# Values of the dilated attention: 512 weight columns per matmul, four PSUM banks held over K pairs

## The chip, the cores and the metric

The kernel runs on one core of a Trainium2 chip. The metric is the device time in microseconds (us). Before the change three runs gave 2682.06, 2686.4 and 2687.64 us; the median is 2686.4 us.

A core has TensorE (PE; its loads of stationary weights are a second row, PEld), VectorE (DVE), ScalarE (ACT), GpSimd (POOL) and SyncE (SP), which issues all DMAs of this kernel in one queue.

## The reference

Two networks of two layers each, one after the other, on a sequence of 512 with 1024 features. The change is in both layers of the first one. There a layer normalizes x to h, multiplies h by `w_in`, and feeds two attentions; cut to what matters here:

```python
p = h @ w_in[layer]                       # h is 512 x 1024
c_q, c_kv, k_r, gate_a, dil_qkv, gate_b = jnp.split(p, split_points, axis=-1)
...
qkv = dil_qkv.reshape(B, S, 3, 3, 8, 64)  # 3 groups, q/k/v, 8 heads of 64
for g, (window, dil) in enumerate(((128, 1), (512, 4), (2048, 16))):
    v = qkv[:, :, g, 2]                   # 512 x 512: the values of group g
    o, lse = banded_attention(to_strided(q, dil), to_strided(k, dil), to_strided(v, dil), ...)
```

So a layer needs three products of 512 x 1024 by 1024 x 512, the values of the three groups. Group 0 uses the rows of v in order; groups 1 and 2 use them with every fourth row together (`to_strided`).

## The kernel before

Everything is kept with features on the 128 partitions: `hh` and `hl` are the high and the low part of h, each [128, 8, 512], where the middle index k counts the eight blocks of 128 features and the last one the tokens. A weight block is loaded as `wraw`, split by ACT into a high part (`whi`, line 75) and by DVE into the rest (`wlo`, line 76), and a product is three matmuls (`mm3`, lines 128 to 132): high by high (L130), high by low (L131), low by high (L132). In the trace's names `out<-a,b` the first name is the operand that streams and the second the stationary one.

For the values the stationary operand is h itself (128 tokens of one feature block), and the weights stream, so that tokens come out on the partitions. Four such sets of 128 tokens, i in the order 1, 2, 3, 0, make up the 512. In group 0 a set is a run of 128 neighbouring tokens (for i = 0 the two ends, copied by POOL into `endq` and `endk`). In groups 1 and 2 set i is `slice(i, 512, 4)`: every fourth token, so the stationary operand is read from `hh` and `hl` with a step of four 4-byte elements.

The loop (lines 564 to 584) runs over six half groups z of 256 weight columns; for each it prefetches the next one's weights (`slabs`, two transfers of 512 KB, alternately in the `whi`/`wlo` buffers and in two buffers `wv`), calls `c.side(VS[z])`, and for each i runs 8 x 3 matmuls into one PSUM bank (`pgv`, pool `pg` of two banks). ACT then scales the result into `v0` or `v12` (line 584).

`c.side(n)` takes n steps of a filler: a step loads 512 KB of another network's modulation weights (`adaw`, line 727) and DVE reduces them (line 728). There are 24 such steps in a layer, and `VS` says how many are placed at which z. The tiles `adaw` use the buffers of `q0` and `k0`, of which `endq` and `endk` hold one each until group 0 is done.

A scheduler puts the instructions of each engine in order when the kernel is built; semaphores then keep the dependences, and each engine runs its own list in order. The matmuls before this stage belong to the other attention (its last product is `po`, line 532), and the scheduler puts some `pgv` matmuls between those. After the stage come the products of q and k (`pg`, weights `in_w_dqk_dram`).

Of the kernel before, what the change touches and what calls it, by code (L numbers as in the profile page):

```python
# [10 lines left out]
F32, F32R, BF16, I32 = dt.float32, dt.float32r, dt.bfloat16, dt.int32  # L11
AF = mybir.ActivationFunctionType
# [5 lines left out]
S = 512  # L18
D = 1024
KD = 8  # L20
# [395 lines left out]
def block1_mixers(c, l, nm, mixf, side, w0, fill):  # L416
    nc, tc = c.nc, c.tc
    hh, hl, rb, rc = nm.hh, nm.hl, nm.rb, nm.rc
    I = c.ins
    W = I["w_in"][l]  # L420
    if True:
# [23 lines left out]
        with ExitStack() as e2:  # L445
# [11 lines left out]
            for ct in range(6):  # L457
                ps = c.gemm(W[:, ct], hh, hl, w=w0.pop(0) if w0 else None, pool=(c.px, "px") if ct in PX else None)
# [15 lines left out]
            for k in (3, 4, 0, 1, 2):  # L474
                t = cf[:, k, :]
# [4 lines left out]
            scale = float(96.0 ** -0.5)  # L480
            khl = [[mp.tile([128, 2, S], F32R, name=f"k{z}{i}") for z in "hl"] for i in range(2)]
            for p in range(4):

                kh, kl = khl[p % 2]
                ps = c.gemm(I["w_uk"][l][:, p], ch[:, 3:5], cl[:, 3:5], 2)
# [9 lines left out]
                for e in range(2):  # L495
                    ps = c.gemm(I["w_uq"][l][:, 2 * p + e], ch, cl, 3)
# [5 lines left out]
                    if (p, e) == (0, 0):  # L502
                        uvh, uvl = c.wslab(I["w_uv"][l], [128, 2, 512])
                        vm = mp.tile([128, 4, 512], F32, name="vm")
                        for i in range(4):
                            ps = (c.px if i in UV else c.pg).tile([128, S], F32, name="pv", tag="px" if i in UV else "pg")
# [29 lines left out]
        with ExitStack() as e2:  # L536
            dp = c.pool(e2, "dil", side)
# [8 lines left out]
            v0 = dp.tile([128, 4, 512], F32, name="v0")  # L546
            v12 = dp.tile([128, 2, 4, 512], F32, name="v12")
            V = I["w_dv"][l]
            ends = [dp.tile([128, KD, 128], F32R, name=f"end{t}", tag=t, bufs=2) for t in ("q0", "k0")]
# [3 lines left out]
            tags = cycle(("q0", "k0"))  # L553
            c.fill.append(fill(lambda: dp.tile([128, 1024], F32, name="adaw", tag=next(tags), bufs=2)))

            def slabs(z):
                ws = []
                for hf in range(2):
                    t = dp.tile([128, 2, 4, 256], F32R, name="wv", tag="qk12", bufs=2) if z % 2 else None
                    ws.append(c.wslab(V[:, z, 4 * hf:4 * hf + 4], [128, 4, 256], out=t and (t[:, 0], t[:, 1])))  # L560
                return ws

            wn = slabs(0)
            for gi in range(3):
                for s in range(2):
                    z = 2 * gi + s
                    wv = wn
                    if z < 5:
                        wn = slabs(z + 1)
                    c.side(VS[z])  # L570
                    cs = slice(256 * s, 256 * s + 256)
                    for i in (1, 2, 3, 0):
                        if gi:
                            h, t, j = (hh, hl), slice(i, 512, 4), 8 + i
                        elif i:
                            h, t, j = (hh, hl), slice(128 * i - 64, 128 * i + 64), 3 + i
                        else:
                            h, t, j = ends, slice(0, 128), 7
                        ps = c.pg.tile([128, 256], F32, name="pgv", tag="pg")
                        for k in range(KD):  # L580
                            wh, wl = wv[k // 4]
                            c.mm3(ps, h[0][:, k, t], h[1][:, k, t], wh[:, k % 4, :], wl[:, k % 4, :], k == 0, k == KD - 1)
                        dst = v0[:, i, cs] if gi == 0 else v12[:, gi - 1, i, cs]
                        nc.scalar.activation(dst, ps, AF.Copy, scale=rc[:, j:j + 1])  # L584
            qk = {}
            top, low = slice(0, 64), slice(64, 128)

# [1012 lines left out]
def build(tc, I, out):  # L1600
    nc = tc.nc
    with ExitStack() as es:
# [62 lines left out]
        for l in range(2):  # L1665
            ex.close()
            prev = nm
            with ExitStack() as em:
                xp = c.pool(em, "mixf", B)
                mixf = xp.tile([128, KD, S], F32, name="mixf")  # L1670
                prev.factors(xp)

                def fill(place):
                    nonlocal sc
                    sc = sc or silu_c(ap)
                    return adaln(c, sc, 0, l, place)

                block1_mixers(c, l, prev, mixf, B, w0 if l == 0 else None, fill)
                mp = c.pool(em, "mp", B)
                if l == 0:  # L1680
                    x = load_x(Scaled, gvec(I["norm_g"][1]))
                else:
                    x = load_x(Norm, *modulation(c, 0, 0, final_g), [I["w_rw"][:, k] for k in range(3)], final_g)
                c.out_proj(mp, I["w_out"][l], 0, [mixf[:, k] for k in range(KD)], x, norm=nm)
            xd = to_dram(xT)
# [195 lines left out]
HB = {0: (0,), 3: (1, 2, 3)}  # L1881
XE = lambda nc: nc.vector
CT = 8
VS = (0, 4, 4, 5, 4, 6)
GT = ((0, 1, 2, 3), (), ())
PX = (2, 3)
UV = (0, 1)
# [60 lines left out]
def slab(w, n=128):  # L1948

    K, N = w.shape  # L1950
    return np.ascontiguousarray(w.reshape(K // 128, 128, N // n, n).transpose(1, 2, 0, 3))


def feat(v):

    v = np.asarray(v)
    return np.ascontiguousarray(np.swapaxes(v.reshape(v.shape[:-1] + (v.shape[-1] // 128, 128)), -1, -2))


def layout_block1(inp):  # L1960
    o = {}
    o["x"] = np.ascontiguousarray(np.asarray(inp["x"])[0].T.reshape(KD, 128, S).transpose(1, 0, 2))
    o["norm_g"] = feat(inp["norm_g"])
    o["final_g"] = feat(inp["final_g"])
    o["qkv_g"] = np.ascontiguousarray(np.concatenate([feat(inp["q_norm_g"]), feat(inp["kv_norm_g"])], -1))
    swp = np.concatenate([np.arange(16, 32), np.arange(0, 16)])
    w_in, w_uk, w_uv, w_uq, w_dv, w_gate, w_dqk, w_out = ([] for _ in range(8))
    for l in range(2):
        w = np.asarray(inp["w_in"][l])
        kr = w[:, 640:672]  # L1970
        w_in.append(slab(np.concatenate([w[:, 0:640], kr, kr, kr[:, swp], kr[:, swp]], 1)))
        w_gate.append(slab(np.concatenate([w[:, 672:1184], w[:, 5792:6304]], 1)))
        dil = w[:, 1184:5792].reshape(1024, 3, 3, 8, 64)
        w_dv.append(slab(np.concatenate([dil[:, g, 2].reshape(1024, 512) for g in range(3)], 1), 256))
        w_dqk.append(slab(np.concatenate([dil[:, g, j, 2 * p:2 * p + 2].reshape(1024, 128)
                                          for p in range(4) for g in range(3) for j in range(2)], 1)))
        ukv = np.asarray(inp["w_ukv"][l]).reshape(256, 8, 128)
        w_uk.append(slab(ukv[:, :, 0:64].reshape(256, 512), 128))
        w_uv.append(slab(ukv[:, :, 64:].reshape(256, 512), 512)[:, 0])
        uq = np.asarray(inp["w_uq"][l]).reshape(384, 8, 96)  # L1980
        cols = []
        for h in range(8):
            n, r = uq[:, h, :64], uq[:, h, 64:]
            cols += [n, r, r[:, swp]] if h % 2 == 0 else [r, r[:, swp], n]
        w_uq.append(slab(np.concatenate(cols, 1)))
        w_out.append(slab(np.asarray(inp["w_out"][l])))
    for k, v in (("w_in", w_in), ("w_uk", w_uk), ("w_uv", w_uv), ("w_uq", w_uq), ("w_dv", w_dv), ("w_gate", w_gate),
                 ("w_dqk", w_dqk), ("w_out", w_out)):
        o[k] = np.stack(v)
    return o  # L1990
# [60 lines left out]
```

## Time and profile before

| | |
|---|---|
| median of three runs | 2686.4 us |
| profiled execution, its own time | 2683.97 us |
| its span | 2682.2 us |
| PE busy | 2589.2 us (97%) |
| DVE, ACT, POOL busy | 63%, 40%, 8% |
| from the last `po` to the first product of q and k, layer 1 | 172.59 to 281.28 us |
| the same, layer 2 | 743.56 to 852.25 us |

A matmul's record has a start that is measured and an end that is modelled, so that records overlap. How fast PE goes is therefore read from the distance between starts.

### The profile page before, as it was taken

How to read it: one execution, taken by the hardware profiler on the slowest of the kernel's cores; microseconds unless marked ns; L12 is line 12 of the kernel's file. 1: busy time of each engine (PE TensorE's matmuls, PEld its weight loads, DVE VectorE, ACT ScalarE, POOL GpSimd, SP SyncE). 2: the span in 40 equal slices, each digit the busy share in tenths (PEclk: the TensorE clock that was granted, in tenths of full speed). 3: DMA queues.
4: the chain of work that ended last, by engine and by line, in shares of the span. 5: the costliest groups of instructions: out<-in, count | busy, mean ns of one | idle time of the engine just before them, and what ended most of it. 6: DMA issues, size and time to landing. Idle time of an engine off the chain costs nothing.

```text
span 2682.2 us, 40139 instructions
## 1 busy us (share of the span) xinstructions
PE 2589.2 (97%) x15813; PEld 2101.0 (78%) x15813; DVE 1685.4 (63%) x3362; ACT 1068.4 (40%) x1923; POOL 220.0 (8%) x311
## 2 busy tenths in 40 slices
PE   8999999999999999999999989899999989999998
PEld 6779877787699777786777777777888867888887
DVE  5773567555844766558668678688454697553544
ACT  5651344434622334554344373532232423432331
POOL 0000111000000111021101123200000210200000
PEclk9999999999999999999998988899999999999999
DMA  4144111241252221331221233388333402233322
GB/s 145 43 166 159 55 56 56 65 144 53 92 189 94 58 61 56 115 99 52 61 72 49 78 111 107 102 260 259 117 95 106 151 26 75 81 89 99 95 82 83
DMA packets 91880, 265.18 MB, mean 99 GB/s; under 512 B 14372, under 2 KB 26924, under 8 KB 90796
## 3 DMA queue, kind: packets, MB, share of 16 engines
q1 hardware_dynamic: 91692, 262.61, 31.3%
q8 instruction: 125, 2.05, 0.3%
q14 instruction: 63, 0.52, 0.1%
HBM read 246.06 MB, written 16.52 MB: 98 GB/s over the span
## 4 chain that ended last, share of the span: by engine, by line
PE 80%; DVE 10%; issue 3%; DMA 3%; ACT 2%; POOL 2%; SPq 0%; ACTq 0%; DVEq 0%; POOLq 0%
PE pg L130 16%; PE pg L131 16%; PE pg L132 16%; PE pgv L132 3%; PE pgv L130 3%; PE pgv L131 3%; DMA adaw<-in_ada_w_dram 2%; DVE wlo L76 2%; PE po L692 1%; PE po L532 1%; PE tp L527 1%; PE sc L632 1%; PE po L697 1%; PE phs L1371 1%; POOL hl L344 1%
## 5 line engine op out<-in xcount | busy, mean ns | idle before, releaser
L130 PE MATMUL pg<-hh,whi 128*128 128x512 f32 x1560 | 632.2, 405 | 9.2 <-ACT whi L124 6.5
L131 PE MATMUL pg<-hl,whi 128*128 128x512 f32 x1560 | 630.5, 404 | 0.0
L132 PE MATMUL pg<-hh,wlo 128*128 128x512 f32 x1560 | 628.4, 403 | 0.3 <-DVE wlo L76 0.3
L75 ACT ACTIVATE whi<-wraw 128x1024 fp32r<-128x1024 f32 (+3 forms) x358 | 335.6, 938 | 695.9 <-PE pg L131 561.1
L76 DVE TENSOR_TENSOR wlo<-wraw,whi 128x1024 fp32r<-128x1024 f32 (+4 forms) x354 | 406.7, 1150 | 295.0 <-ACT whi L75 289.4
L130 PEld LDWEIGHTS pg<-hh,whi 128*128 128x128 f32 x1560 | 295.9, 190 | 86.1 <-ACT whi L124 6.5
L131 PEld LDWEIGHTS pg<-hl,whi 128*128 128x128 f32 x1560 | 296.6, 190 | 76.5 <-issue 7.5
L132 PEld LDWEIGHTS pg<-hh,wlo 128*128 128x128 f32 x1560 | 296.4, 190 | 76.4 <-issue 6.1
L130 PE MATMUL pg<-hidh,whi 128*128 128x512 f32 (+1 forms) x396 | 147.3, 372 | 0.0
L131 PE MATMUL pg<-hidl,whi 128*128 128x512 f32 (+1 forms) x396 | 146.7, 370 | 0.0
L132 PE MATMUL pg<-hidh,wlo 128*128 128x512 f32 (+1 forms) x396 | 146.1, 369 | 0.0
L728 DVE CUSTOM_DVE_ANT_0 adaw<-adaw,sc 128x1024 f32<-128x1024 f32 x96 | 116.6, 1225 | 44.4 <-DMA adaw<-in_ada_w_dram 37.3
L600 POOL TENSOR_TENSOR shf<-shf,roped 128x512 f32<-128x512 f32 x48 | 61.9, 1289 | 622.0 <-ACT whi L75 339.1
L584 ACT ACTIVATE v<-pgv,rsy 128x256 f32<-128x256 f32 x48 | 22.8, 474 | 166.7 <-PE pgv L132 162.8
L132 PEld LDWEIGHTS pg<-hidh,wlo 128*128 128x128 f32 x396 | 74.4, 188 | 14.5
L130 PEld LDWEIGHTS pg<-hidh,whi 128*128 128x128 f32 x396 | 74.4, 188 | 14.2
L641 ACT ACTIVATE pp<-pp,nm 128x256 f32<-128x256 f32 x128 | 63.5, 497 | 54.6 <-DVE nm L638 54.6
L131 PEld LDWEIGHTS pg<-hidl,whi 128*128 128x128 f32 x396 | 74.4, 188 | 13.7
L131 PE MATMUL pgv<-wlo,hh 128*128 128x256 f32 x240 | 83.9, 350 | 0.0
L130 PE MATMUL pgv<-whi,hh 128*128 128x256 f32 x240 | 83.9, 350 | 0.0
L132 PE MATMUL pgv<-whi,hl 128*128 128x256 f32 x240 | 83.6, 348 | 0.0
L1541 ACT ACTIVATE fu<-fu 128x512 f32<-128x512 f32 x44 | 27.8, 632 | 112.6 <-DVE fu L754 112.6
(540 smaller groups left out, 4947.9 us busy)
## 6 DMA issues: line engine op xcount, KB each, us to landing
adaw<-in_ada_w_dram SPq DMA_DIRECT2D x96, 512.0 KB, 4.6
wraw<-in_ffn_up_dram SPq DMA_DIRECT2D x88, 512.0 KB, 3.6
wraw<-in_w_dqk_dram SPq DMA_DIRECT2D x48, 512.0 KB, 3.5
wraw<-in_ffn_down_dram SPq DMA_DIRECT2D x32, 512.0 KB, 3.6
wraw<-in_w_dv_dram SPq DMA_DIRECT2D x24, 512.0 KB, 3.8
wraw<-in_w_gate_dram SPq DMA_DIRECT2D x16, 512.0 KB, 3.7
wraw<-in_w_out_dram SPq DMA_DIRECT2D x16, 512.0 KB, 3.8
wraw<-in_w_hg_dram SPq DMA_DIRECT2D x16, 512.0 KB, 3.7
```

Of the source, the lines that this page charges most:

```text
L75: nc.scalar.activation(hi, raw, AF.Copy)
L76: (eng or nc.vector).tensor_tensor(lo, raw, hi.bitcast(F32), op=ALU.subtract)
L130: mm(out, lhsT=ah, rhs=bh, start=first, stop=False)
L131: mm(out, lhsT=ah, rhs=bl, start=False, stop=False)
L132: mm(out, lhsT=al, rhs=bh, start=False, stop=last)
L344: nc.gpsimd.tensor_tensor(self.hl[:, k, t], u, h, op=ALU.subtract)
L527: nc.tensor.transpose(tp[:, kt, :], pe[:, kt * 128:(kt + 1) * 128], c.ident)
L532: nc.tensor.matmul(po[64 * e:64 * e + 64], lhsT=vm[:, kt, p * 128 + 64 * e:p * 128 + 64 * e + 64], rhs=pts[e][:, kt, :], start=kt == 0, st ...
L600: nc.gpsimd.tensor_tensor(sh, sh, roped[:, 1, :], op=ALU.mult)
L641: nc.scalar.activation(pz, pz, AF.Exp, bias=nm[:, z, i:i + 1], scale=0.125, accum_out=st[:, 1, z, i:i + 1])
L728: nc.vector.tensor_tensor_reduce(w, in0=w, in1=sc, scale=1.0, scalar=0.0, op0=ALU.mult, op1=ALU.add, accum_out=mod[:, j:j + 1])
L1541: nc.scalar.activation(u, u, AF.Silu)
```

## The change

The values of a group are now made in one go: each matmul streams 512 weight columns instead of 256. The loop runs over the three groups and, inside, over four K pairs (`kp`, two feature blocks each); the weights of a pair are one transfer of 512 KB in the ordinary `whi`/`wlo` buffers. Since all four sets i are still open when the next pair comes, four PSUM banks are held over the group: those of `pg` and `px` for groups 0 and 2, those of `py` and `pz` for group 1. ACT evicts the four banks at the end of a group. The weights are laid out in blocks of 512 columns, and `VS` now has twelve entries.

```diff
-            def slabs(z):
-                ws = []
-                for hf in range(2):
-                    t = dp.tile([128, 2, 4, 256], F32R, name="wv", tag="qk12", bufs=2) if z % 2 else None
-                    ws.append(c.wslab(V[:, z, 4 * hf:4 * hf + 4], [128, 4, 256], out=t and (t[:, 0], t[:, 1])))
-                return ws
-
-            wn = slabs(0)
             for gi in range(3):
-                for s in range(2):
-                    z = 2 * gi + s
-                    wv = wn
-                    if z < 5:
-                        wn = slabs(z + 1)
-                    c.side(VS[z])
-                    cs = slice(256 * s, 256 * s + 256)
+                pools = ((c.pg, "pg"), (c.px, "px")) if gi % 2 == 0 else ((c.py, "py"), (c.pz, "pz"))
+                ps = [pools[i // 2][0].tile([128, S], F32, name="pgv", tag=pools[i // 2][1]) for i in range(4)]
+                for kp in range(4):
+                    wh, wl = c.wslab(V[:, gi, 2 * kp:2 * kp + 2], [128, 2, S])
+                    c.side(VS[4 * gi + kp])
                     for i in (1, 2, 3, 0):
                         if gi:
-                            h, t, j = (hh, hl), slice(i, 512, 4), 8 + i
+                            h, t = (hh, hl), slice(i, 512, 4)
...
-                        ps = c.pg.tile([128, 256], F32, name="pgv", tag="pg")
-                        for k in range(KD):
-                            wh, wl = wv[k // 4]
-                            c.mm3(ps, h[0][:, k, t], h[1][:, k, t], wh[:, k % 4, :], wl[:, k % 4, :], k == 0, k == KD - 1)
-                        dst = v0[:, i, cs] if gi == 0 else v12[:, gi - 1, i, cs]
-                        nc.scalar.activation(dst, ps, AF.Copy, scale=rc[:, j:j + 1])
+                        for j in range(2):
+                            k = 2 * kp + j
+                            c.mm3(ps[i], h[0][:, k, t], h[1][:, k, t], wh[:, j, :], wl[:, j, :], k == 0, k == KD - 1)
+                for i in (1, 2, 3, 0):
+                    j = 8 + i if gi else 3 + i if i else 7
+                    nc.scalar.activation(v12[:, gi - 1, i] if gi else v0[:, i], ps[i], AF.Copy, scale=rc[:, j:j + 1])
...
-VS = (0, 4, 4, 5, 4, 6)
+VS = (0, 2, 2, 2, 2, 2, 2, 2, 2, 3, 2, 2)
```

The built order changes in this stage of the two layers and in the end of the attention before it; elsewhere all engines' lists are the same. Three places follow, each from the first layer.

SP's queue from the first `adaw` transfer to the second transfer for q and k, before:

```order
L727 DMA adaw<-in_ada_w_dram 128x1024 x2
L67 DMA wraw<-in_w_dv_dram 128x1024
L727 DMA adaw<-in_ada_w_dram 128x1024
L67 DMA wraw<-in_w_dv_dram 128x1024
L727 DMA adaw<-in_ada_w_dram 128x1024 x2
L67 DMA wraw<-in_w_dv_dram 128x1024
L727 DMA adaw<-in_ada_w_dram 128x1024 x3
L67 DMA wraw<-in_w_dv_dram 128x1024
L727 DMA adaw<-in_ada_w_dram 128x1024 x5
L67 DMA wraw<-in_w_dv_dram 128x1024 x2
L727 DMA adaw<-in_ada_w_dram 128x1024 x10
L67 DMA wraw<-in_w_dqk_dram 128x1024
```

and now:

```order
L718 DMA adaw<-in_ada_w_dram 128x1024 x2
L67 DMA wraw<-in_w_dv_dram 128x1024 x2
L718 DMA adaw<-in_ada_w_dram 128x1024 x2
L67 DMA wraw<-in_w_dv_dram 128x1024
L718 DMA adaw<-in_ada_w_dram 128x1024 x12
L67 DMA wraw<-in_w_dv_dram 128x1024
L718 DMA adaw<-in_ada_w_dram 128x1024 x3
L67 DMA wraw<-in_w_dv_dram 128x1024
L718 DMA adaw<-in_ada_w_dram 128x1024 x2
L67 DMA wraw<-in_w_dv_dram 128x1024
L718 DMA adaw<-in_ada_w_dram 128x1024 x2
L67 DMA wraw<-in_w_dqk_dram 128x1024
```

Six of the twelve `w_dv` transfers of the layer stand ahead of these rows in both. Of the other six, three (the last three K pairs of group 2) now come behind a run of twelve `adaw` transfers.

ACT's list from the first split after the attention (`whi` and `wv` are splits of weights, `v` are evictions), before:

```order
L75 ACTIVATE wv<-wraw 128x1024 x2
L584 ACTIVATE v_1512<-pgv,rsy 128x256 x3
L75 ACTIVATE whi<-wraw 128x1024
L584 ACTIVATE v_1512<-pgv,rsy 128x256 x4
L75 ACTIVATE wv<-wraw 128x1024
L75 ACTIVATE whi<-wraw 128x1024
L584 ACTIVATE v_1512<-pgv,rsy 128x256
L75 ACTIVATE wv<-wraw 128x1024
L584 ACTIVATE v_1513<-pgv,rsy 128x256 x3
```

and now:

```order
L75 ACTIVATE whi<-wraw 128x1024 x3
L575 ACTIVATE v_1512<-pgv,rsy 128x512 x4
L75 ACTIVATE whi<-wraw 128x1024 x3
L575 ACTIVATE v_1513<-pgv,rsy 128x512 x4
L75 ACTIVATE whi<-wraw 128x1024 x4
L575 ACTIVATE v_1513<-pgv,rsy 128x512 x2
L75 ACTIVATE whi<-wraw 128x1024
L575 ACTIVATE v_1513<-pgv,rsy 128x512 x2
```

The evictions of a group now stand in one run (the last one in two). The splits for the next group's first two pairs stand ahead of group 0's run, the split for group 2's first pair ahead of group 1's run.

PE at the end of group 2 and the first product of q and k (numbers are tiles: `pgv_1824` is set i = 0), before:

```order
L130 MATMUL pgv_2259<-wv_2042,hh_103 128x256
L131 MATMUL pgv_2259<-wv_2042,hh_103 128x256
L132 MATMUL pgv_2259<-wv_2042,hl_104 128x256
L130 MATMUL pg_2299<-hh_103,whi_2291 128x512
L131 MATMUL pg_2299<-hl_104,whi_2291 128x512
```

and now:

```order
L130 MATMUL pgv_1824<-whi_1941,hh_103 128x512
L131 MATMUL pgv_1824<-wlo_1942,hh_103 128x512
L132 MATMUL pgv_1824<-whi_1941,hl_104 128x512
L130 MATMUL pg_1993<-hh_103,whi_1985 128x512
L131 MATMUL pg_1993<-hl_104,whi_1985 128x512
```

Width and buffers have changed; the order of the two stages has not. The bank given to `pg_1993` is that of set i = 1 (`pgv_1825`), the first of the four to be finished and evicted.

## Rows read from the trace of the kernel before

**Rows 1.** The page: busy time of PE, and the chain by engine and line.
```profile
PE 2589.2 (97%) x15813; PEld 2101.0 (78%) x15813; DVE 1685.4 (63%) x3362; ACT 1068.4 (40%) x1923; POOL 220.0 (8%) x311
...
PE 80%; DVE 10%; issue 3%; DMA 3%; ACT 2%; POOL 2%; SPq 0%; ACTq 0%; DVEq 0%; POOLq 0%
PE pg L130 16%; PE pg L131 16%; PE pg L132 16%; PE pgv L132 3%; PE pgv L130 3%; PE pgv L131 3%; DMA adaw<-in_ada_w_dram 2%; DVE wlo L76 2%; PE po L692 1%; PE po L532 1%; PE tp L527 1%; PE sc L632 1%; PE po L697 1%; PE phs L1371 1%; POOL hl L344 1%
```
**Rows 2.** Windows: attention's end, then the stage in both layers (columns named in the header).
```profile
core 0: us, PE busy (x) PEld busy (x) DVE busy (x) ACT busy (x) POOL busy (x), PEclk, DMA share, GB/s
151.40:172.59 21.19, 21.10 (x116) 12.67 (x114) 12.77 (x34) 13.87 (x29) 1.05 (x2) 1.00 0.40 150
172.59:281.28 108.69, 108.69 (x545) 108.69 (x545) 44.95 (x65) 20.73 (x33) 0.00 (x0) 1.00 0.48 165
743.56:852.25 108.69, 108.69 (x545) 108.69 (x545) 44.80 (x64) 20.74 (x33) 0.00 (x0) 1.00 0.49 165
```
**Rows 3.** Timeline of PE, group 0, 256 columns (start us, length us).
```profile
182.06 0.28 PE L130 MATMUL pgv<-wv,hh 128*128 128x256 f32 x1
...
182.77 0.28 PE L130 MATMUL pgv<-wv,hh 128*128 128x256 f32 x1
```
**Rows 4.** The same, group 1: 256 columns, stationary operand with step four.
```profile
211.97 0.40 PE L130 MATMUL pgv<-whi,hh 128*128 128x256 f32 x1
...
212.67 0.40 PE L130 MATMUL pgv<-whi,hh 128*128 128x256 f32 x1
```
**Rows 5.** The same, first product of q and k: 512 columns, no step.
```profile
281.28 0.39 PE L130 MATMUL pg<-hh,whi 128*128 128x512 f32 x1
...
281.98 0.39 PE L130 MATMUL pg<-hh,whi 128*128 128x512 f32 x1
```
**Rows 6.** Windows of the `pgv` instructions alone: groups 1 and 2 of layer 1.
```profile
191.67:281.28 89.61, 89.61 (x386) 89.57 (x384) 7.58 (x16) 1.00 0.46 158
```
**Rows 7.** Timeline of PEld: line 378, one streamed column; without step, then step four.
```profile
21.75 1.53 PEld L378 LDWEIGHTS pst<-ones,sqa 128*128 128x128 f32 x13
...
23.51 1.94 PEld L378 LDWEIGHTS pst<-ones,sqa 128*128 128x128 f32 x8
```
**Rows 8.** The instructions of the tile `pst` of line 378: shortest/median/longest in ns.
```profile
L378 PEld LDWEIGHTS pst<-ones,sqa x52: 133/192/330, 21.5 to 591.6; 128*128 128x128 f32 x44, 128*64 128x64 f32 x8
```
**Rows 9.** Groups by line, 172.6 to 281.3 us: busy us, mean ns, idle before.
```profile
L728 DVE CUSTOM_DVE_ANT_0 adaw<-adaw,sc 128x1024 f32<-128x1024 f32 x24 | 28.8, 1221 | 8.2 <-DMA adaw<-in_ada_w_dram 8.1
L584 ACT ACTIVATE v<-pgv,rsy 128x256 f32<-128x256 f32 x23 | 10.9, 475 | 78.2 <-PE pgv L132 76.3 <-PE po L532 1.9
L76 DVE TENSOR_TENSOR wlo<-wraw,whi 128x1024 fp32r<-128x1024 f32 x6 | 7.3, 1225 | 24.7 <-ACT whi L75 24.7
L75 ACT ACTIVATE whi<-wraw 128x1024 fp32r<-128x1024 f32 x6 | 6.3, 1051 | 3.3 <-PE pgv L132 3.3
```
**Rows 10.** Groups of ACT, 140 to 172 us: a copy of 512 columns out of PSUM.
```profile
L528 ACT ACTIVATE ptm<-tp 128x512 f32<-128x512 f32 x14 | 8.3, 598 | 8.2 <-PE tp L527 8.2
```
**Rows 11.** DMA view, 172.6 to 281.3 us: GB/s in 40 slices, total, issue to landing (us).
```profile
GB/s 0 193 176 216 274 270 238 240 342 338 381 366 369 274 3 14 304 345 302 0 0 6 0 0 193 176 309 317 341 15 0 193 6 188 5 193 0 0 0 0
DMA packets 4901, 17.90 MB, mean 165 GB/s; under 512 B 544, under 2 KB 544, under 8 KB 4896
...
adaw<-in_ada_w_dram SPq DMA_DIRECT2D x22, 512.0 KB, 5.0
```
**Rows 12.** Windows, layer 1: GB/s is the last column.
```profile
200.00:220.00 20.00, 20.00 (x87) 20.00 (x87) 10.52 (x17) 2.61 (x5) 0.00 (x0) 1.00 0.67 249
```
**Rows 13.** SP's queue: timeline, and waits of 172.6 to 281.3 (us, times, longest).
```profile
202.59 39.41 SPq L727 DMA_DIRECT2D adaw<-in_ada_w_dram  x10
...
SPq L727 <- DVE mod L728: 55.1, 20, 17.0
```

More of the change, by code (lines that the diff above doesn't have):

```diff
@@ L572, in block1_mixers @@
                     for i in (1, 2, 3, 0):
                         if gi:
-                            h, t, j = (hh, hl), slice(i, 512, 4), 8 + i
+                            h, t = (hh, hl), slice(i, 512, 4)
                         elif i:
-                            h, t, j = (hh, hl), slice(128 * i - 64, 128 * i + 64), 3 + i
+                            h, t = (hh, hl), slice(128 * i - 64, 128 * i + 64)
                         else:
-                            h, t, j = ends, slice(0, 128), 7
@@ L579, in block1_mixers @@
-                        ps = c.pg.tile([128, 256], F32, name="pgv", tag="pg")
-                        for k in range(KD):
-                            wh, wl = wv[k // 4]
-                            c.mm3(ps, h[0][:, k, t], h[1][:, k, t], wh[:, k % 4, :], wl[:, k % 4, :], k == 0, k == KD - 1)
-                        dst = v0[:, i, cs] if gi == 0 else v12[:, gi - 1, i, cs]
-                        nc.scalar.activation(dst, ps, AF.Copy, scale=rc[:, j:j + 1])
+                            h, t = ends, slice(0, 128)
@@ L1973, in layout_block1 @@
         dil = w[:, 1184:5792].reshape(1024, 3, 3, 8, 64)
-        w_dv.append(slab(np.concatenate([dil[:, g, 2].reshape(1024, 512) for g in range(3)], 1), 256))
+        w_dv.append(slab(np.concatenate([dil[:, g, 2].reshape(1024, 512) for g in range(3)], 1), 512))
         w_dqk.append(slab(np.concatenate([dil[:, g, j, 2 * p:2 * p + 2].reshape(1024, 128)
```

## The prediction

> **What bounds the kernel now.** I read the page first: PE is busy for 97% of the span and holds 80% of the chain that ended last; in its list by line the products of the values (`pgv`) stand behind those of the shared product helper (`pg`), with 3% for each of their three lines [rows 1]. So PE's own time is what a change must cut. Then the windows of the two stages that the change touches: 108.69 us in each layer, PE and PEld busy throughout, granted clock 1.00 (the 2.4 GHz level), DMA at half its share, DVE 45 us and ACT 21 us busy [rows 2]. Nobody makes PE wait there.
>
> What PE does in that time is read from starts. In group 0, where the stationary operand is contiguous, six matmuls of 256 columns take 0.71 us: 118 ns each [rows 3]. In groups 1 and 2, where it is read with a step of four elements, three take 0.70 us: 233 ns each, for the same 256 columns [rows 4]. A matmul of 512 columns with a contiguous stationary operand also takes 233 ns [rows 5]. So in groups 1 and 2 something other than the columns sets the pace. Line 378 says what: it streams a single column per matmul, and its loads follow each other by (1.53 - 0.19) / 12 = 112 ns when contiguous and by (1.94 - 0.33) / 7 = 230 ns with a step of four [rows 7]; the lengths of one load, 192 and 330 ns, are those of its own group [rows 8]. A strided load takes about 233 ns whether one column or 256 stream beside it. PE in groups 1 and 2 is bound by loads, and half of its streaming time is empty: 384 loads in 89.61 us [rows 6].
>
> **The change part by part**, for one layer; both layers have the same counts and the same 108.69 us.
>
> *Groups 1 and 2.* Before: 2 groups x 2 halves x 4 sets x 8 blocks x 3 = 384 matmuls, each with its load, 89.6 us [rows 6]. After: 2 x 4 sets x 8 blocks x 3 = 192, with 512 columns. No row shows a strided load beside 512 columns. Lower bound: the longer of load and stream, 233 ns [rows 4, 5], 44.8 us. Upper bound: none of the second 256 columns is hidden, 233 + 117 = 350 ns, 67.2 us. I take 234.5 ns, near the lower end: the nearest row is the contiguous case, where a load of 112 ns beside a stream of about 117 gives 118 [rows 3, 7], so two nearly equal lengths cost a nanosecond over the longer one. 192 x 234.5 = 45.0 us; the term is -44.6 us (bounds -44.8 and -22.4).
>
> The Trainium skill ("TensorE: Matmul & The Clock Gate", LDWEIGHTS) gives a load as columns / 1.2, an estimate of 107 ns for these 128, with no word of a step. By it loads would be hidden in 118 ns already, halving their number would gain nothing, and the sum would be about 0. The rows say otherwise, 230 ns [rows 7], and decide.
>
> *Group 0.* 192 x 118 ns = 22.6 us become 96 x 233 ns = 22.4 us: -0.2 us [rows 3, 5].
>
> *Evictions.* 24 of 475 ns [rows 9] become 12 of 512 columns, each like ACT's 598 ns copy [rows 10]. ACT is busy for 20.73 of 108.69 us, and in a group the bank of i = 1 is finished three sets (18 matmuls, 4.2 us) before the last. Group 1 has banks of its own, so PE does not stop between groups. Group 2 needs group 0's banks back, a whole group (22 us) later. The first product of q and k takes the bank of i = 1, free by then: 0. Had it been the last bank, it would be 0.6 us and a semaphore.
>
> *Weights.* The same 12 transfers and splits. A transfer now feeds 24 matmuls of 0.2345 us, 5.6 us of PE; before it fed 48, 5.7 us in group 0 and 11.2 in groups 1 and 2. The list of SP now has twelve `adaw` transfers ahead of the second pair of group 2. Worked by hand, from the end of group 0 as zero: ACT evicts until 0.8, splits group 1's third pair until 1.9, DVE follows until 3.1 and can only then reduce again. DVE's reductions (1.2 us each [rows 9]) and the splits, which wait for a weight buffer that PE frees every 5.6 us, then stand in turn: split at 6.8 to 8.0, three reductions to 11.8, split to 13.6, six reductions to 21. SP issues the twelfth `adaw` at 16.1, when the one four back is reduced, and the weights right behind it; with about 4 to 5 us to land [rows 11] they are there at 21. ACT is then busy with group 1's evictions until 23.2, splits until 24.3, DVE until 25.5. PE needs them at 22.5 + 5.6 = 28. The margin is 2.5 us; the pairs behind have 3 to 5. So 0, with up to 5 us if supply is thin: 17.90 MB [rows 11] in 61 us are 294 GB/s; slices of the stage reach 338 to 381 [rows 11].
>
> *The end of the attention before.* There 32 matmuls of 256 columns (3.8 us) filled PE's gaps; now 28 of 512 (6.5 us) do, and DVE and ACT do the same three splits in another place. All of this is counted in the terms above if the gaps have no room; PE is busy for 21.10 of 21.19 us there [rows 2], modelled ends included, so little room. If the 2.7 us all fitted, that would be -2.7. If the splits, now earlier, push the softmax chain, at most one more of each is in its way (1.05 + 1.22 us [rows 9]): +2.3. I take +0.5.
>
> *Sum.* -44.6 - 0.2 + 0.5 = -44.3 us a layer, -88.6 us for two. Against the profiled execution's own 2683.97 us (span 2682.2 and 1.8 around it) that is 2595.4; the median of the runs is 2.4 above that execution, so 2597.8 us.
>
> **The rivals.**
>
> 1. *Load and stream hide each other only in part.* 233 ns for 256 columns is also 2 x 117. If a strided load of 117 ns ran ahead of its stream instead of beside it, 512 columns would take 350 ns, and the layer would gain 22.4 + 0.2 - 0.5 = 22.1 us: 2642 us. Against it: with one column the distance is 230 ns too [rows 7], where the sum would be about 117. The Trainium skill ("TensorE: Matmul & The Clock Gate", The mechanism) says that a load overlaps a running matmul only when they use different row groups, which would put every load here in series. By that rule, the trace disagrees: contiguous loads of 112 ns and streams of 117 make 118 together [rows 3, 7].
>
> 2. *Supply becomes the bound.* All of the stage's 17.90 MB now have to come in 61 us. At the 249 GB/s of one stretch of the stage before [rows 12] they take 71.9, which is 11.0 more a layer: 2 x 33.3 = 66.6 us gained, 2620 us. For it: DVE already waits 8.1 us for `adaw` [rows 9], and only four buffers hold them, two until group 0 is done. Against it: 249 is a stretch in which SP waited for DVE, not for the engines.
>
> 3. *Slower: the twelve `adaw` issues in a row.* PE's second pair of group 2 stands behind them in SP's queue. The row of ten before took 39.4 us, 3.9 per issue, and SP waited 55.1 us for DVE's reductions in 20 waits, 17.0 at longest [rows 13]. At 3.9 the weights would be issued 44 us after group 0 and ready at 51, 23 us late, which eats half of the gain. The run begins 3.3 us before the end of group 0, and landing and splits take 5.0 + 1.05 + 1.14, so from (28 + 44.3 - 7.2 + 3.3) / 12 = 5.7 us per issue the kernel is slower than before. If every second issue waited as long as the longest, 8.5 each, PE would stand still for 78 us, 34 more than the gain: 2684 + 67 + 2 = 2753 us. Against it: these waits were paced by weight buffers, of which PE freed one per 11.2 us; it now frees one per 5.6.
>
> 4. *No change*, 2686 us: loads are not what sets the pace in groups 1 and 2 (233 ns would then belong to the columns read there, and 512 of them would take 467), against the 230 ns beside one column [rows 7]. The rule on a load's length in the Trainium skill, above, would come out here too.
>
> **How the numbers follow.** Forecast 0.82, rival 1 0.05, rival 2 (any part of it) 0.09, rival 3 0.02, rival 4 0.02. The forecast's own range: at best 44.8 + 0.2 + 2.7 = 47.7 a layer, 2591 us, at worst 44.6 + 0.2 - 2.3 - 3 = 39.5, 2607; the runs shown spread by 4 us below their median, so it begins at 2588. To leave no more than 2 in 10 outside, the range takes in rival 2 and ends at 2622. About 0.2% (5 us) is what a measurement of this kernel tells from no change. Faster by more: all but rivals 3 and 4, 0.96; within it: rival 4, 0.02; slower: rival 3, 0.02.
>
> **What would show it.** Right: the distance between `pgv` starts in groups 1 and 2 stays at 233 to 236 ns with 512 columns; from the last `po` to the first product of q and k there are about 61 us instead of 108.69, granted clock 1.00; PE is nowhere idle in it; the rest of the program has its old lengths. Wrong: starts 300 ns or more apart (rival 1); idle PE ahead of the second to fourth K pair of group 2, released by `wlo` or `whi`, with SP waiting for DVE (rivals 2 and 3); the attention's end, 21.19 us before, longer by more than 5 us; or a granted clock below 1.00 in a stage where it was not.

## The result, and the profile after

The changed kernel takes 2590.61 us (median of four runs, 2589.3 to 2591.42), the kernel before 2685.08 us: a ratio of 0.9648, 95% interval 0.9631 to 0.9665. The forecast was 2597.8 us. The profiled execution took 2591.42 us, with a span of 2589.6.

The page of the profile after, PE's busy time and the chain by engine and line, which answer to [rows 1]:

```profile
PE 2495.2 (96%) x15237; PEld 1999.1 (77%) x15237; DVE 1685.8 (65%) x3362; ACT 1063.7 (41%) x1899; POOL 219.6 (8%) x311
...
PE 82%; DVE 9%; ACT 2%; issue 2%; DMA 2%; POOL 2%; SPq 0%; ACTq 0%; DVEq 0%; POOLq 0%
PE pg L130 18%; PE pg L131 18%; PE pg L132 18%; DMA adaw<-in_ada_w_dram 2%; PE pgv L130 2%; PE pgv L132 2%; PE pgv L131 2%; PE po L683 1%; PE po L532 1%; DVE wlo L76 1%; PE tp L527 1%; PE sc L623 1%; PE po L688 1%; POOL hl L344 1%; PE phs L1362 1%
```

PE has 576 matmuls fewer and is busy 94 us less; DVE's work is the same and ACT's 5 us less. The `pgv` lines fell from 3% of the chain to 2% each.

The windows of [rows 2], now for the changed kernel: the attention's end, then the stage in the first and in the second layer.

```profile
core 0: us, PE busy (x) PEld busy (x) DVE busy (x) ACT busy (x) POOL busy (x), PEclk, DMA share, GB/s
150.58:173.92 23.34, 23.34 (x112) 13.55 (x110) 12.97 (x34) 12.05 (x27) 1.05 (x2) 1.00 0.36 135
173.92:235.82 61.90, 61.90 (x261) 58.94 (x261) 43.46 (x64) 18.81 (x22) 0.00 (x0) 1.00 0.76 272
700.08:761.98 61.90, 61.90 (x261) 58.94 (x261) 43.53 (x63) 18.93 (x22) 0.00 (x0) 1.00 0.77 272
```

The stage fell from 108.69 to 61.90 us in each layer, PE still busy all the time at a granted clock of 1.00; the attention's end grew from 21.19 to 23.34, since more of the work lies in it. Together, from the first `pgv` matmul to the first product of q and k, 129.88 us became 85.24: 44.64 a layer. PEld is now idle for 3 of 61.9 us, nearly all of it in group 0; in groups 1 and 2 loads and streams are almost in balance. In the timeline of PE, group 1 of the changed kernel, against [rows 4]:

```profile
190.24 0.40 PE L132 MATMUL pgv<-whi,hl 128*128 128x512 f32 x1
190.47 0.41 PE L130 MATMUL pgv<-whi,hh 128*128 128x512 f32 x1
190.72 0.40 PE L131 MATMUL pgv<-wlo,hh 128*128 128x512 f32 x1
190.95 0.41 PE L132 MATMUL pgv<-whi,hl 128*128 128x512 f32 x1
191.20 0.40 PE L130 MATMUL pgv<-whi,hh 128*128 128x512 f32 x1
```

Starts are about 234 and 247 ns apart in turn, whichever of the three products it is. The window of groups 1 and 2, `pgv` alone (the length, then busy time of PE, PEld and ACT, clock, DMA share, GB/s), gives the mean, 46.06 / 192 = 239.9 ns, for twice the columns that took 233 before [rows 6]:

```profile
189.76:235.82 46.06, 46.06 (x193) 45.91 (x192) 5.51 (x8) 1.00 0.86 315
```

The queue of SP and the weights were the forecast's tightest place. SP's timeline and, below it, DVE's split of the second K pair of group 2 (timeline of DVE):

```profile
189.68 16.76 SPq L718 DMA_DIRECT2D adaw<-in_ada_w_dram  x12
206.53 0.38 SPq L67 DMA_DIRECT2D wraw<-in_w_dv_dram  x1
```

```profile
214.67 1.23 DVE L76 TENSOR_TENSOR wlo<-wraw,whi 128x1024 fp32r<-128x1024 f32 x1 [1.93 <-ACT whi L75]
```

The twelve `adaw` issues took 1.40 us each, where the row of ten before took 3.9 [rows 13]. The pair was split at 215.90; PE wanted it 24 matmuls after 212.80, at 218.56: 2.7 us to spare, 2.5 forecast.

### The profile page after: what moved, and what is told of

It is laid out like the page before. It is cut to its first block, busy times and chain, and to the rows that moved or that the text cites. A ratio compares the mean times of both kernels' runs of the same rounds, so it can differ in the third digit from the quotient of the medians.

```text
span 2589.6 us, 38979 instructions
## 1 busy us (share of the span) xinstructions
PE 2495.2 (96%) x15237; PEld 1999.1 (77%) x15237; DVE 1685.8 (65%) x3362; ACT 1063.7 (41%) x1899; POOL 219.6 (8%) x311
## 4 chain that ended last, share of the span: by engine, by line
PE 82%; DVE 9%; ACT 2%; issue 2%; DMA 2%; POOL 2%; SPq 0%; ACTq 0%; DVEq 0%; POOLq 0%
PE pg L130 18%; PE pg L131 18%; PE pg L132 18%; DMA adaw<-in_ada_w_dram 2%; PE pgv L130 2%; PE pgv L132 2%; PE pgv L131 2%; PE po L683 1%; PE po L532 1%; DVE wlo L76 1%; PE tp L527 1%; PE sc L623 1%; PE po L688 1%; POOL hl L344 1%; PE phs L1362 1%
## 5 line engine op out<-in xcount | busy, mean ns | idle before, releaser
L75 ACT ACTIVATE whi<-wraw 128x1024 fp32r<-128x1024 f32 (+3 forms) x370 | 348.1, 942 | 749.2 <-PE pg L131 561.0
L76 DVE TENSOR_TENSOR wlo<-wraw,whi 128x1024 fp32r<-128x1024 f32 (+4 forms) x366 | 421.5, 1153 | 271.3 <-ACT whi L75 264.9
L131 PE MATMUL pgv<-wlo,hh 128*128 128x512 f32 (+1 forms) x240 | 91.0, 379 | 0.0
L130 PE MATMUL pgv<-whi,hh 128*128 128x512 f32 (+1 forms) x240 | 90.4, 376 | 0.0
L132 PE MATMUL pgv<-whi,hl 128*128 128x512 f32 (+1 forms) x240 | 89.9, 375 | 0.0
L231 DVE SCALAR_TENSOR_TENSOR xT<-pg,mod,xT 128x512 f32<-128x512 f32 (+1 forms) x54 | 38.4, 710 | 50.5 <-PE pg L132 50.4
```

The costliest lines, as they stand in the source:

```text
L75: nc.scalar.activation(hi, raw, AF.Copy)
L76: (eng or nc.vector).tensor_tensor(lo, raw, hi.bitcast(F32), op=ALU.subtract)
L130: mm(out, lhsT=ah, rhs=bh, start=first, stop=False)
L131: mm(out, lhsT=ah, rhs=bl, start=False, stop=False)
L132: mm(out, lhsT=al, rhs=bh, start=False, stop=last)
L231: self.nc.vector.scalar_tensor_tensor(x, in0=ps, scalar=gate[:, o:o + 1], in1=x, op0=ALU.mult, op1=ALU.add)
```

## The experiments

Stretches are told for one layer; where only one number stands, both layers agree within 0.1 us. "Before group 1" is the stretch from the first `pgv` matmul to the first of group 1: 40.27 us before (21.19 + 19.08), 39.18 after.

**The load is what bound it.** The kernel before, with neighbouring tokens:

```diff
-                            h, t, j = (hh, hl), slice(i, 512, 4), 8 + i
+                            h, t, j = (hh, hl), slice(128 * i, 128 * i + 128), 8 + i
```

> The kernel before, 256 columns, but groups 1 and 2 take 128 neighbouring tokens per set in place of every fourth, so the values of these groups are of other tokens than the reference's. Theory (the strided load of the stationary operand sets the pace): the 384 matmuls of groups 1 and 2 come 118 ns apart, as in group 0, instead of 233; the stage from the last po to the first product of q and k falls from 108.7 to about 64 us in each layer, the whole to about 2596 us (ratio 0.967), the same gain as the change gave. If the supply of weights can't follow at twice the pace, up to 5 us a layer of PE idle ahead of a wlo. Rival (the pace belongs to the columns or to what streams): 233 ns and 108.7 us stay, 2685 us.

2600.6 us, ratio 0.9698 (0.9681 to 0.9715). Timeline of PE and windows of groups 1 and 2, layers 1 and 2:

```profile
199.96 0.28 PE L130 MATMUL pgv<-whi,hh 128*128 128x256 f32 x1
200.08 0.28 PE L131 MATMUL pgv<-wlo,hh 128*128 128x256 f32 x1
...
200.31 0.28 PE L130 MATMUL pgv<-whi,hh 128*128 128x256 f32 x1
```

```profile
190.77:236.36 45.59, 45.59 (x387) 45.40 (x386) 33.55 (x50) 15.00 (x24) 0.00 (x0) 1.00 0.89 311
719.13:765.64 46.51, 45.85 (x387) 45.45 (x386) 33.52 (x49) 14.99 (x24) 0.00 (x0) 1.00 0.87 303
```

With 256 columns and the old loop, the step alone gives 44.0 and 43.1 us a layer. Rival 4 of the prediction (the pace belongs to the columns) is out. In layer 2 PE waits once, 0.5 us, for an eviction to free its bank: at twice the pace two banks of `pg` are not always enough.

**What is left of the load beside 512 columns.** The same edit in the changed kernel.

> The changed kernel, 512 columns, with 128 neighbouring tokens per set in groups 1 and 2 (values of other tokens than the reference's). Theory (with 512 columns the stream sets the pace, and the strided load beside it costs only the 13 ns on every second matmul that the changed kernel shows): distances of 233 to 234 ns without the alternation of 234 and 247, 192 x 6 ns = 1.2 us less a layer, 2588 us (ratio 0.964). Rival (load and stream share in part, so that a shorter load gives more): distances stay near 240, or the load's 120 ns come back and the stage falls by far more than 2 us. Second rival (the alternation has to do with the banks or with which product it is): 234 and 247 stay with the contiguous load.

2586.93 us, 0.9641 (0.9627 to 0.9655). Groups 1 and 2, `pgv` alone:

```profile
189.01:232.96 43.95, 43.95 (x193) 35.87 (x191) 5.49 (x8) 1.00 0.91 329
```

43.95 / 192 = 228.9 ns, without the alternation. So the step costs 11 ns per matmul beside 512 columns and 115 beside 256 (233.4 - 118.7 in the kernel above). The alternation goes with the step, not with the bank or the product (the second rival is out), and the load is hidden but for these 11 ns. They are 2.1 us a layer, more than the 1.2 expected, since the stream alone takes 229 ns and not 233.

**The width alone undone.**

```diff
-                            c.mm3(ps[i], ..., wh[:, j, :], wl[:, j, :], k == 0, k == KD - 1)
+                            for hf, q in enumerate(HALVES):
+                                c.mm3(ps[i][:, q], ..., wh[:, j, q], wl[:, j, q],
+                                      k == 0 and hf == 0, k == KD - 1 and hf == 1)
```

> The changed kernel with its K pairs and four held banks, but each matmul of 512 columns done as two of 256 (the stationary operand loaded for each): the width alone is undone. Theory (only the number of strided loads counts): the pace in groups 1 and 2 is 233 ns for 256 columns again, 384 of them, the stage is back at 108 to 109 us, the whole at 2682 to 2688 us. Rival (the four banks, the K pairs or the new order of transfers give part of the gain): the stage stays well under 108 us; each tenth of the gain kept that way would be 9 us.

2684.14 us, 0.9999 (0.9988 to 1.001). Groups 1 and 2:

```profile
190.96:280.56 89.60, 89.60 (x386) 89.56 (x384) 5.51 (x8) 1.00 0.46 162
```

The 89.6 us of [rows 6] to a hundredth, with four held banks, K pairs and the new transfers. These give nothing by themselves but 0.3 us before group 1.

**The two parts apart.** Group 0 in the new manner and groups 1 and 2 in the old one, then the other way round; the other loop stands beside it over the groups left out:

```diff
-            for gi in range(3):
+            for gi in range(1):
                 pools = ((c.pg, "pg"), (c.px, "px")) if gi % 2 == 0 else ((c.py, "py"), (c.pz, "pz"))
...
-            for gi in range(3):
+            for gi in range(1, 3):
                 for s in range(2):
```

> Group 0 alone in the new manner (512 columns, four banks over K pairs); groups 1 and 2 in the old one, with 256 columns per matmul (their weights now read in rows of 1 KB out of the layout of 512 columns). Theory by the terms of the prediction: 96 x 233 ns in place of 192 x 118 gives -0.2 us a layer, the end of the attention +0.5, so no change, 2685 us within 0.2%. From the trace of the changed kernel, where group 0 ended 1.9 us earlier in layer 1 and 1.1 in layer 2, a theory of its own: the wider matmuls fill gaps of PE in the attention's end, and about 3 us of the 94.5 come from there: 2682 us. Rival (a larger part of the gain comes from group 0 and the attention's end): more than 5 us faster.

2680.87 us, 0.9984 (0.9972 to 0.9996): by the whole hardly a difference, so the stretches decide. The `pgv` instructions in the attention's end, in the rest of group 0, and in groups 1 and 2; then the first two of these stretches in the kernel before:

```profile
151.40:174.75 23.35, 7.96 (x28) 4.95 (x29) 0.00 (x0) 1.00 0.37 135
174.75:190.59 15.84, 15.84 (x69) 12.92 (x69) 2.03 (x3) 1.00 0.46 144
190.59:280.08 89.49, 89.49 (x385) 89.45 (x384) 7.82 (x16) 1.00 0.50 174
```

```profile
151.40:172.59 21.19, 5.18 (x33) 4.23 (x33) 0.00 (x0) 1.00 0.40 150
172.59:191.67 19.08, 19.08 (x161) 19.08 (x161) 3.33 (x7) 1.00 0.60 195
```

> Groups 1 and 2 alone in the new manner, group 0 in the old one with 256 columns (its weights in rows of 1 KB). Theory (the terms add up: group 0 alone gave 1.06 us a layer in the stretch before group 1, and nothing in groups 1 and 2): groups 1 and 2 take 46.06 us in place of 89.6, the stretch before group 1 stays at 118.5, the whole falls by about 2 x 43.5 = 87 us, to 2597 us (ratio 0.967 to 0.968). Rival (the parts need each other, by the banks or the order of transfers): PE idle ahead of group 1, or less than 80 us gained.

2597.44 us, 0.9679 (0.9659 to 0.9699). From the first `pgv` to the first product of q and k: 128.67 us with group 0 alone (-1.21), 86.53 with groups 1 and 2 alone (-43.35). The sum, -44.56, is the whole (-44.64): the parts don't need each other. The part of group 0 is PE's gaps: 28 matmuls of 512 columns lie in the attention's end in place of 32 of 256, so 24 x 119 ns = 2.9 us more work in a stretch that is 2.16 us longer.

**Which steps cost.** Step two in group 1 and step eight in group 2 (over two feature blocks), in either kernel:

```diff
-                            h, t = (hh, hl), slice(i, 512, 4)
+                            h, t = (hh, hl), slice(i % 2 + 256 * (i // 2), 256 * (i // 2) + 256, 2)
...
+                            if gi == 2:
+                                e = slice(1024 * (k // 2) + 4 * (k % 2) + i, 1024 * (k // 2) + 1024, 8)
+                                ah, al = hf8[0][:, e], hf8[1][:, e]
```

> The kernel before, 256 columns, with the step of the stationary operand changed: two elements in group 1, eight in group 2 (over two feature blocks), so the values of these groups are not the reference's. Streams of 117 ns leave a longer load in full view. Theory (an element of its own per 16 bytes is what costs): step two brings two elements of every 16 bytes, the distance is 118 ns as without a step and group 1 takes 22.7 us in place of 44.8; step eight costs what step four costs, 233 ns and 44.8 us. The sum: 44 us less over two layers, about 2640 us. The Trainium skill (SBUF - State Buffer) says at least two hits in a 16-byte line are wanted for full bandwidth; by that rule the first is so. Rival (cost grows with the step): step two near 150 to 175 ns, step eight well over 233.

2642.74 us, one run. Windows of group 1 and group 2, 192 matmuls each:

```profile
190.15:213.19 23.04, 23.04 (x194) 23.04 (x193) 3.78 (x8) 1.00 0.95 343
213.19:259.59 46.40, 46.40 (x194) 46.36 (x192) 3.81 (x8) 1.00 0.38 132
```

Step two: 120 ns, two more than without a step [rows 3]. Step eight: 241.7, eight more than step four. Nearly the theory: the cost comes at once between two and four elements, not in proportion. The Trainium skill ("SBUF — State Buffer", Specifications (TRN2)) has 16-byte cachelines that want two hits each for full bandwidth; by that rule step two of 4-byte elements is free and step four is not, and the trace agrees, 120 against 233 ns. The 8 ns from four to eight it does not tell.

> The changed kernel, 512 columns, with step two in group 1 and step eight in group 2 (values not the reference's). Theory (with 512 columns only a load about as long as the stream shows): group 1 with step two at the pace of the contiguous operand, 229 ns, group 2 with step eight at the pace of step four, 240 ns on average with 234 and 247 in turn; 22.0 and 23.0 us. Rival (any step disturbs the stream, whatever the load's length): group 1 near 240 as well. If step eight loads take longer than 247 ns, group 2 goes at the load's own pace.

2589.08 us, one run. Groups 1 and 2:

```profile
188.70:211.11 22.41, 22.41 (x98) 18.76 (x97) 2.76 (x4) 1.00 0.92 321
211.11:234.61 23.50, 23.50 (x97) 23.35 (x96) 2.75 (x4) 1.00 0.80 305
```

233.4 and 244.8 ns a matmul, against 228.9 without a step and 239.9 with step four. Neither story holds whole: a load of at most 120 ns (step two above), far shorter than the stream, still costs 4.5 ns, so the longer of load and stream is not all that counts. What adds these few nanoseconds is open.

**The margin in SP's queue.** All 23 fillers that `VS` places, at one place:

```diff
-VS = (0, 2, 2, 2, 2, 2, 2, 2, 2, 3, 2, 2)
+VS = (0, 0, 0, 0, 0, 0, 0, 23, 0, 0, 0, 0)
```

> The changed kernel with all 23 filler steps of a layer placed at the last K pair of group 1, so that 19 adaw transfers in a row stand ahead of the last three transfers of w_dv, in place of twelve. In the changed kernel the twelve took 16.8 us of SP, 1.4 each, and the weights of the second pair of group 2 were split 2.7 us before PE wanted them. Theory (that margin is real, and a queue's order is what spends it): seven more issues of 1.4 us come 9.8 us later, less what ACT's evictions no longer hold up; PE stands still 4 to 8 us a layer ahead of the second pair of group 2, released by wlo, and nowhere else in the stage; 2599 to 2607 us. Rival (the margin was larger than it looked, or the scheduler's places don't decide): no idle PE, 2590 us. Rival of the prediction (issues cost 5.7 us and more): 40 us a layer, 2670 us.

2612.43 us, 0.9742 (0.9727 to 0.9756). SP's timeline and its waits of 189 to 219 us (us, times, longest), then PE's timeline, in layer 1:

```profile
189.77 27.47 SPq L718 DMA_DIRECT2D adaw<-in_ada_w_dram  x19
217.34 1.61 SPq L67 DMA_DIRECT2D wraw<-in_w_dv_dram  x3
...
SPq L718 <- DVE mod L719: 22.0, 16, 4.4
```

```profile
218.54 0.39 PE L132 MATMUL pgv<-whi,hl 128*128 128x512 f32 x1
225.09 1.24 PE L130 MATMUL pgv<-whi,hh 128*128 128x512 f32 x2 [6.15 <-ACT whi L75]
226.35 0.81 PE L131 MATMUL pgv<-wlo,hh 128*128 128x512 f32 x1
226.96 0.63 PE L132 MATMUL pgv<-whi,hl 128*128 128x512 f32 x1
227.38 0.63 PE L130 MATMUL pgv<-whi,hh 128*128 128x512 f32 x1
```

Windows of group 1 and around the stop (all engines, columns as above):

```profile
190.00:213.03 23.03, 23.03 (x97) 23.03 (x97) 18.76 (x29) 5.83 (x7) 0.00 (x0) 1.00 0.90 320
...
218.50:225.10 6.60, 0.45 (x3) 0.14 (x2) 4.24 (x9) 1.06 (x1) 0.00 (x0) 0.75 0.98 375
225.10:229.00 3.90, 3.88 (x9) 2.74 (x10) 3.76 (x4) 2.12 (x2) 0.00 (x0) 0.55 0.81 290
229.00:244.24 15.24, 15.24 (x65) 15.20 (x64) 4.00 (x7) 4.19 (x5) 0.00 (x0) 1.00 0.42 139
```

The margin is real: counted from the start of group 1, the weights were issued 10.6 us later than in the changed kernel (27.34 against 16.77 us), and PE stood still for 6.2 us at the expected place and nowhere else in this layer. The idle row names `whi`, not the `wlo` expected: both are late, the first matmul wants `whi`. Each issue took 1.45 us. SP spent 22.0 of those 27.5 us waiting for DVE's reductions; DVE was busy for 18.76 of 23.03 us of group 1, the DMA engines for 0.90 of it at 320 GB/s. Which of the two sets this pace is not shown. The whole cost more than forecast, 8.2 us in layer 1 and 11.0 in layer 2, for two reasons: the stop was longer in layer 2 (starts 9.1 us apart), and after each stop the granted clock is down, as the second window shows (0.55): starts are 610 to 650 ns apart, of which a wait for `wlo` is a part, and then 427, until it is 1.00 again some 4 us later.

**A version that takes the 11 ns back.** hh is copied once a layer into the order of the sets, in buffers that `wv` left free; `hl` keeps its step.

```diff
+            hps = [dp.tile([128, 4, 4, 128], F32R, name="hp", tag="qk12", bufs=2) for _ in range(2)]
+            for k in range(KD):
+                nc.gpsimd.tensor_copy(hps[k // 4][:, k % 4], hh[:, k, :].rearrange("p (n i) -> p i n", i=4).bitcast(F32))
...
+                            ah = hps[k // 4][:, k % 4, i] if gi else h[0][:, k, t]
```

> The changed kernel with a copy of hh in the order of the sets, made by POOL in 8 instructions of 128x512 in the buffers that wv left free, so that two of three stationary operands of groups 1 and 2 (high by high, high by low) are contiguous; hl keeps its step. Theory (the contiguous 512-column pace is 229 ns and the step costs 11 ns on average): a single strided load between two contiguous ones is hidden, the distances fall from 240 to 229 to 233 ns, 192 x 7 to 11 ns = 1.3 to 2.1 us a layer, 2586.5 to 2588 us against 2590.6, if POOL's copies (about 10 us, after the copies of the ends) are done before group 1. Rival (copies of POOL slow DVE or come too late): the attention's end is longer by 1 to 5 us a layer, and nothing or less is left.

2592.25 us, 0.9668 (0.9652 to 0.9684): no gain. Groups 1 and 2 do go at 233.4 ns (44.81 us), but the stretch before group 1 is 40.68 us in place of 39.18. POOL's row (timeline), DVE's lines of the attention's end and three rows of DVE's timeline tell why:

```profile
152.15 10.63 POOL L559 CAST hp<-hh 128x512 fp32r<-128x512 f32 x8
```

```profile
L524 DVE TENSOR_SCALAR pe<-pe,mst 128x512 f32<-128x512 f32 x8 | 6.9, 863 | 0.2
...
L125 DVE TENSOR_TENSOR ql<-qf,qh 128x512 fp32r<-128x512 f32 x1 | 1.6, 1606 | 0.0
```

```profile
153.39 1.24 DVE L524 TENSOR_SCALAR pe<-pe,mst 128x512 f32<-128x512 f32 x1
...
157.94 1.35 DVE L519 TENSOR_REDUCE mst<-sc 128x1 f32<-128x512 f32 x2
...
165.38 0.49 DVE L524 TENSOR_SCALAR pe<-pe,mst 128x512 f32<-128x512 f32 x1
```

The scaling of line 524, on the softmax chain that PE waits for, takes 863 ns on average in place of 487: 1.15 to 1.41 us in the four that lie beside POOL's copies, 0.49 in the four behind them. The reduction of line 519, which reads PSUM, keeps its 0.68 us beside them.

The copies on ACT instead, behind the last softmax copy:

```diff
-                nc.gpsimd.tensor_copy(hps[k // 4][:, k % 4], hh[:, k, :].rearrange("p (n i) -> p i n", i=4).bitcast(F32))
+                    for k in range(KD) if gi == 0 and kp == 3 else ():
+                        nc.scalar.activation(hps[k // 4][:, k % 4], hh[:, k, :].bitcast(F32).rearrange("p (n i) -> p i n", i=4), AF.Copy)
```

> As perm_hh, but the eight copies of hh are made by ACT behind the last softmax copy of the attention, six ahead of the first split of the stage and two behind it. With POOL's copies the pace in groups 1 and 2 fell from 239.9 to 233.4 ns, 1.25 us a layer, and DVE's scaling in the attention's end (line 524) went from 487 to 863 ns beside them, which made that stretch 1.5 us longer. Theory (POOL's copies slow DVE; ACT's don't, and ACT has 4 us free before the first split): the pace stays at 233.4 ns, line 524 at 487 ns, the stretch before group 1 at 117.4 us, and the kernel is 2.5 us faster than the changed one, about 2588 us: less than the runs can tell, so the stretches of the trace decide. Rival (ACT's copies push the splits, 8 x 0.6 us): PE waits up to 1 us a layer ahead of the last K pair of group 0.

The same two lines of DVE, and the window of groups 1 and 2 (`pgv` alone):

```profile
L524 DVE TENSOR_SCALAR pe<-pe,mst 128x512 f32<-128x512 f32 x8 | 3.9, 487 | 0.2
...
L125 DVE TENSOR_TENSOR ql<-qf,qh 128x512 fp32r<-128x512 f32 x1 | 0.7, 684 | 0.0
```

```profile
190.59:235.40 44.81, 44.81 (x193) 39.13 (x191) 5.51 (x8) 1.00 0.90 321
```

Beside it the changed kernel ran once more, with no edit.

> The changed kernel once more, beside perm_act: 2590.6 us by the first runs, with stretches of 117.4 us before group 1 and 46.06 us in groups 1 and 2, in both layers. If perm_act gains, this one is 2 to 3 us slower than it.

2588.56 us against 2591.17 of the changed kernel, ratios 0.9651 (0.9635 to 0.9668) and 0.9663 (0.9647 to 0.9679): the runs can't tell them apart. The stretches can: from the first `pgv` to the first product of q and k 83.99 and 84.07 us, where the changed kernel has 85.24 in both profiles. ACT's copies give 1.2 us a layer, about 2.4 of 2591: the pace of groups 1 and 2 falls to 233.4 ns and the stretch before them stays at 39.18 us. So this version is ahead of the changed kernel in these stretches, by less than a measurement of the whole shows.

## Why the prediction was right

*The bound.* Right, and now shown: taking the step away does what the change does, and undoing the width alone gives all of it back.

*Groups 1 and 2*, forecast -44.6: measured 89.61 - 46.06 = -43.55. The mechanism was right and the size off by 1.0 us: 239.9 ns a matmul in place of 234.5. I had added one nanosecond to the longer of two nearly equal lengths, after the pair of 112 and 117; the pair of 230 and 229 costs 10.

*Group 0 and the attention's end*, forecast -0.2 + 0.5: measured 39.18 - 40.27 = -1.09. The bounds of the end held this (-2.7 to +2.3), the value taken had the wrong sign: the split that might have pushed the softmax chain did not, and 0.7 us of the wider matmuls went into gaps of PE. Busy for 21.10 of 21.19 us had looked like no room; modelled ends, as the prediction noted, hide such gaps. The pace gave the other 0.4: the 136 halves left in group 0 would have taken 136 x 119 = 16.2 us and take 15.84.

*Evictions and weights*, forecast 0: PE has no idle time in the stage. The margin of 2.7 us was forecast as 2.5, and not by luck: counted from the end of group 0, the weights were issued at 16.8 us (forecast 16.1), split at 26.1 (25.5) and wanted at 28.8 (28). The kernel with 19 issues in a row shows what lies behind it. Rival 3 had the right place and the wrong price: 1.4 us per issue, not 3.9 to 8.5, lower as its own counter-argument said. Rival 2's 249 GB/s was no bound: groups 1 and 2 ran at 315.

*The sum*, forecast -44.3 a layer: measured -44.64. That they agree within 0.4 us is luck: errors of +1.0 and -1.4 cancel. Two layers are 89.3 us; the profiled executions differ by 92.55. The other 3.3 us lie outside the two stretches: there 2422.4 us became 2419.1. The changed kernel's second profile has 2415.8 for the same work with the same stretches, and the kernel with groups 1 and 2 alone 2427.6; the mean granted clocks of these three profiles are 0.977, 0.978 and 0.975. So this rest moves by more than 3 us from run to run, and none of it is shown to belong to the change. The forecast of 2597.8 us was 7.2 too high: 0.7 comes from the two stretches, 3.3 from this rest, and 3.2 from the step from the profiled execution to the median, taken as +2.4 and measured as -0.8.

## What to carry to other kernels

Where a stationary operand is read with a step, look at the distance between starts for one streamed column and for many: if it is the same, the load is the bound, and wider matmuls (fewer loads) give what an operand without a step would. Once load and stream are of one length, a few per cent over the longer one can remain (239.9 ns against 230 here). When a stage becomes twice as fast, recompute from the new pace how late each transfer in a shared queue comes; old waiting times there were set by the old pace.

## What the runs showed of the hardware

With 256 columns, matmuls whose stationary operand is read with steps of one, two, four and eight 4-byte elements come 118, 120, 233 and 242 ns apart. ACT pays for the step too: its copy of 512 elements with step four took 1.12 us (the lines of tile `hp` in the kernel with ACT's copies), against 0.63 of the same copy without a step, a weight split of the same kernel. Both go from SBUF to SBUF:

```profile
L75 ACT ACTIVATE whi<-wraw 128x512 fp32r<-128x512 f32 x32 | 20.1, 627 | 34.3 <-PE pg L131 30.2 <-DVE rst L142 3.3 <-ACT whi L75 0.4
...
L565 ACT ACTIVATE hp<-hh x16: 1094/1124/1147, 170.8 to 707.9; 128x512 fp32r<-128x512 f32 x16
```

Copies on POOL more than doubled the time of two kinds of DVE instruction beside them (0.49 to between 1.15 and 1.41 us for line 524, 0.68 to 1.61 for line 125), and left the reduction out of PSUM (line 519, 0.68) as it was; what sets the two apart is not shown. And a stop of PE of 6.2 us cost 8.2, about a third more than itself: afterwards the granted clock was mostly at the 1.2 GHz level (0.55 in the window) for a few microseconds, with 427 ns between starts of 512 columns.
